# A hybrid decoder trunk: probabilities turned as one tile, gate sums by scans on VectorE, and a fifth weight buffer

## The chip, the cores and the metric

The kernel runs on one core of one Trainium2 chip. The metric is the device time of one execution in microseconds (us). The core has TensorE (PE, matrix products), VectorE (DVE), ScalarE (ACT), GpSimd (POOL) and SyncE (SP); SP, ACT and POOL also issue DMAs, which 16 DMA engines carry out.

## What is computed

The trunk has two layers over 256 rows of width 2048. In each layer the input is normalised and multiplied with one wide matrix (`w_in`), whose columns feed four groups of four heads; the groups' outputs, each times its own SiLU gate, are concatenated, multiplied with `w_out` and added to the input. One more normalisation follows the last layer.

```
h = rms_norm(x, norm_g);  p = split_columns(h @ w_in)
fox  = softmax(q.k/sqrt(d) + F[t] - F[s], causal) v,   F = cumsum(log_sigmoid(f))
diff = (softmax(q1.k1) - lam * softmax(q2.k2)) v, then rms_norm
moba = softmax(q.k, causal) v        (one block of 256 keys, so all of it is the own block)
gla  = sum over s <= t of (q_t * exp(C[t] - C[s])) . k_s v_s, then rms_norm
       C = cumsum(log_sigmoid(a @ wa + ba)) / 16, for each of 64 features of a head
x = x + concat(fox, diff, moba, gla, each * silu(gate)) @ w_out
```

Everything is float32.

## The kernel before

**Weights.** Each product with `w_in` or `w_out` is made in blocks of up to 512 columns and in steps of two or four 128-row pieces. A step loads 512 KB of weights from memory into a `raw` buffer (`load`, L1116, on SP's queue, `RAW_BUFS` = 4 of them), splits them into a part `hi` on ACT (`hi_of`, L414) and a rest `lo` on DVE (`lo_of`, L417), and multiplies: activations are also split in two (`hTp`, or `mTh` and `mTl`), and three products hi·hi, lo·hi, hi·lo add up in PSUM (`multiply`, L1196; an ordinary step is 12 matmuls of 512 columns). Parts are made three steps ahead (`ahead`, L1249).

**Order.** The order of all instructions on every engine is written by the program itself. The main loop (L1282) goes through the steps; behind each step `tick` (L263) lets every pending task go on to its next `yield`. Tasks are Python generators: `gla`, `fox`, `diff`, `moba`, the `run` that follows a projection, `make_hT` at the layer's end. So a `yield` means "behind the next step of 12 matmuls". `tick` stops when a rough count of the DVE or ACT time given out exceeds what PE has had (`Costed`, L169; `give_time`, L1242). A step that needs something not ready yet forces ticks (L1290).

**Buffers.** Working tiles come from numbered slots: `four` (4 KB a partition, `T4` = 10), `two` (2 KB, `T2` = 6), `eight` (one), `gate` (two) and `side` (two, in PSUM). `take` waits in steps for a free one.

**Turning.** A 128x128 transpose of float32 data is made off PE: DVE transposes 32x32 blocks (`turned`, L289), and two DMA hops on POOL's queue put the blocks in their places by way of DRAM (`moved`, L303): the first hop writes a tile `turn`, two yields later four DMAs read it back, and three yields later the tile counts as landed. The softmax probabilities of a group are two tiles, of the first 128 queries (4 blocks, in a `two` slot) and of the second (8 blocks, in a `four` slot); `turned_p` (L775) turns both as two jobs, which makes 2 + 8 DMAs. In MoBA and FoX the product of probabilities and values (`attend_columns`, L794) reads the turned tiles directly; in diff they are copied first (L984).

**GLA.** `gla` (L625) needs exp of differences of the running sum C at seven levels of halving blocks, for both halves of 128 rows, and two whole-half sums. Before, each is a sum of log gates over a set of rows: a constant matrix `a_r` of nine 128x128 sets is multiplied with the log gates, split in hi and lo (`gh`, `glo`), on PE (L661 to L672), and ACT takes exp out of PSUM into `ee` (L674). Then DVE multiplies with q and k (L683 to L696) and PE makes the products of `ee` and `tq` (L701).

**The layer's end.** `make_hT` (L447) turns the new `xs` into the next layer's `hTp` in four chunks; the first three by `moved`, the last by PE transposes (`turn_x`, L426). The output projection takes its inputs in the order GLA, FoX, diff, MoBA.

Of the kernel before, what the change touches and what calls it, by code (L numbers as in the profile page):

```python
# [21 lines left out]
P = 128  # L22
# [11 lines left out]
NEG = -1.0e30  # L34
RAW_BUFS = 4
PART_BUFS = 4
WARM = 10
X_AT = (24, 28, 32, 36)
T4 = 10
T2 = 6  # L40
STEP_W = 1056
# [21 lines left out]
def _constants():  # L63

    i = np.arange(P)
    tables, at = {"f": [], "b": []}, {}

    def put(name, a, kind="f"):
        parts = tables[kind]
        at[name] = (sum(x.shape[1] for x in parts), a.shape[1])  # L70
        parts.append(np.ascontiguousarray(a, TYPES[kind]))

    put("ident", np.eye(P))
    put("after", (i[:, None] > i[None, :]))
# [9 lines left out]
    sets, masks = [], []  # L84
    for h in GLA_LEVELS:
        blk, second = i // (2 * h), (i // h) % 2 == 1
        ref = blk * 2 * h + h - 1
        u, t = i[:, None], i[None, :]
        a = np.where(second[None, :], (u > ref[None, :]) & (u <= t), (u > t) & (u <= ref[None, :]))
        sets.append(a / GLA_TAU)  # L90
        masks.append(((blk[:, None] == blk[None, :]) & ~second[:, None])[:, second])
    sets += [(i[:, None] > i[None, :]) / GLA_TAU, (i[:, None] <= i[None, :]) / GLA_TAU]
    put("sets", np.concatenate(sets, 1), "b")
    put("masks", np.concatenate(masks, 1), "b")
    return {k: np.concatenate(v, 1) for k, v in tables.items()}, at
# [115 lines left out]
def hybrid_trunk(  # L211
# [30 lines left out]

    s4 = Slots(wk, "four", T4)
    s2 = Slots(wk, "two", T2)
    s8 = Slots(wk, "eight", 1)
    sgs = Slots(wk, "gate", 2)
# [41 lines left out]

    def turned(jobs, release):  # L289

        made = []
        for src, slots, inner in jobs:
            n = src.shape[1]
            t = yield from slots.take([P, 4, n, 32] if inner == "j" else [P, 4, 32, n])
            v_.transpose(t.rearrange("p c n j -> p n c j" if inner == "j" else "p c j n -> p n c j"),
                         src.rearrange("p n (c i) -> p n c i", c=4))
            made.append(t)
        release()
        yield
        yield from moved(made)  # L300
        return made

    def moved(made):  # L303

        via = []
        for t in made:
            n = t.shape[2] * t.shape[3]
            via.append(dram.tile([P, 4, n], F32, name=f"turn{n}", tag=f"turn{n}", bufs=4))
            g_.dma_start(via[-1], t.rearrange("p c a b -> p c (a b)"))  # L309
        yield  # L310
        yield
        for t, z in zip(made, via):
            for c in range(4):
                g_.dma_start(t[c * 32:(c + 1) * 32].rearrange("p q a b -> p q (a b)"), z[:, c].rearrange("(q i) e -> i q e", q=4))  # L314
        yield
        yield
        yield

# [16 lines left out]
    ones_r = cp.tile([P, P], F32R, name="ones_r")  # L335
    a_r = cp.tile([P, (NL + 2) * P], F32R, name="a_r")
    neg_b = cp.tile([P, P], BF16, name="neg_b")
# [23 lines left out]
    def constants():  # L361
# [5 lines left out]
        s = []  # L367
        for name in ("sets", "upto", "masks"):
# [11 lines left out]
        yield  # L380
        v_.tensor_copy(a_r, s[0])
        v_.tensor_copy(upto_r, s[1])
        v_.tensor_copy(masks.rearrange("p l t -> p (l t)"), s[2])
        v_.tensor_scalar(ones_r, ident, 0.0, 1.0, op0=OP.mult, op1=OP.add)
# [62 lines left out]
    def make_hT(l, chunk, parts):  # L447
        if chunk < 3:
            yield
        if l == 1 and chunk < 2:  # L450
# [3 lines left out]
            for _ in range(4):  # L454
                yield
        if chunk == 3:
            ps = yield from take_side()
            turn_x(ps, chunk)
            yield
            split_x([ps[:, k * 256:(k + 1) * 256].rearrange("p (m t) -> p m t", m=2) for k in range(4)], l, chunk)  # L460
            side.put(ps)
            yield
            squares(l, chunk, parts)
            return
# [3 lines left out]
        for m in range(2):  # L468
            v_.transpose(tk[:, m], x4[:, m].rearrange("p k (c i) -> p k c i", c=4))
        yield  # L470
        squares(l, chunk, parts)
        yield from moved([t])
        tk = t.rearrange("p q j (k m) -> p k m (q j)", m=2)
# [30 lines left out]
    def projected(name, pool=None, heads_first=False, func=AF.Copy, turn=None, natural=None):  # L504
# [7 lines left out]
        def run(l, nat):  # L512
            yield
            if turn is not None:
                yield from rotated(nat, *turn)
            t, = yield from turned([(nat, pool or s4, "j")], lambda: s4.put(nat))
            if natural:
# [39 lines left out]
    def finish_rows(l, gi, o, ops, scale, sg):  # L557
# [20 lines left out]
        yield  # L578
        t, = yield from turned([(mixed.rearrange("p h m d -> p (h m) d"), s4, "j")], lambda: s4.put(mixed))
        z = yield from natural_of(t, s4, ((slice(None), gain[:, 0 if gi == 1 else 1, l:l + 1]),))  # L580
# [44 lines left out]
    def gla(l, an):  # L625
        yield from until("constants")
        ps = yield from take_side()
        for m in range(2):
# [5 lines left out]
        al = yield from take_side()  # L634
        for m in range(2):
            matmul(al[:, m * 256:(m + 1) * 256], at17[:, m * P:(m + 1) * P], wa[:, l], True, True)
        yield
        e = yield from s2.take([P, 512])
        gl = yield from s2.take([P, 2, 256])
        yield from log_sigmoid(gl.rearrange("p m e -> p (m e)"), al[:, :512], e)  # L640
        s2.put(e)
        side.put(al)
        yield
        gh = yield from s2.take([P, 2, 256], F32R)
        hi_of(gh, gl)
        yield
        glo = yield from s2.take([P, 2, 256], F32R)
        lo_of(glo, gl, gh)
        s2.put(gl)
# [9 lines left out]
        for pair in range(2):  # L659
            ee = yield from s8.take([P, 2, NL + 1, P])  # L660
            for m in range(2):  # L661
                pe = yield from take_side()
                for b in range(2):
                    for part in (gh, glo):
                        lhs = part[:, m, pair * P:(pair + 1) * P]
                        if b == 0:
                            matmul(pe[:, :512], lhs, a_r[:, 0:512], part is gh, part is glo)
                        elif m == 0:
                            matmul(pe[:, 512:], lhs, a_r[:, 512:1024], part is gh, part is glo)
                        else:  # L670
                            matmul(pe[:, 512:896], lhs, a_r[:, 512:896], part is gh, False)
                            matmul(pe[:, 896:], lhs, a_r[:, (NL + 1) * P:], False, part is glo)  # L672
                yield
                a_.activation(ee[:, m].rearrange("p l t -> p (l t)"), pe, AF.Exp)  # L674
                side.put(pe)
            yield

# [40 lines left out]
        s4.put(env["gla_qk", l])  # L718
        s2.put(gh, glo)
        yield from until(("gla_v", l))  # L720
# [53 lines left out]

    def turned_p(p0, p1, inner, pool0=s2, slot0=None):  # L775

        def release():
            pool0.put(p0 if slot0 is None else slot0)
            s4.put(p1)

        t0, t1 = yield from turned([(p0, s2, inner), (p1.rearrange("p h j s -> p (h j) s"), s4, inner)], release)
        return t0, t1

    def normalised(p0, p1, su):
# [6 lines left out]
        yield  # L791
        return (yield from turned_p(p0, p1, "j"))

    def attend_columns(l, gi, name, qT, kT, forget=None):  # L794
# [3 lines left out]
        yield  # L798
        t0, t1 = yield from normalised(p0, p1, su)
        yield from until((name + "_v", l))  # L800
# [5 lines left out]
        for h in range(H):  # L806
            v0, v1 = vn[:, 0, h * P:(h + 1) * P], vn[:, 1, h * P:(h + 1) * P]
            matmul(o[:, h, :P], v0, t0[:, :, h], True, True)
            matmul(o[:, h, P:], v0, t1[:, :, 2 * h], True, False)
            matmul(o[:, h, P:], v1, t1[:, :, 2 * h + 1], False, True)  # L810
        s4.put(t1, vn)
        s2.put(t0)
        yield
# [94 lines left out]
    def diff(l):  # L908
# [73 lines left out]
        s4.put(p1[1])  # L982
        t0, t1 = yield from turned_p(p0[:, 0], p1[0], "j", s4, p0)
        z0 = yield from natural_of(t0, s2)  # L984
        z1 = yield from natural_of(t1, s4)
        yield
# [343 lines left out]
```

## Time and profile before

| | |
|---|---|
| runs, us | 942.41, 937.63, 938.47 (median 938.47) |
| the profiled execution, us | 939.94; its span from the first to the last instruction 938.1 |
| busy: PE, DVE, ACT, POOL, us | 917.3, 577.6, 505.5, 120.5 |
| DMA | 204.56 MB, 218 GB/s on average |
| granted clock of PE, mean | 0.991 |

The profile is of one execution. Its first part gives each engine's busy time and share of the span. Lines of groups and of the timeline read: start or group, engine, operation, tile written `<-` tiles read, shapes, number of instructions, and in square brackets the idle time before the instruction and who ended it. Buffer numbers are left out, so `four` is any tile in a `four` slot; `gate<-turn` is the second hop of a tile in a `gate` slot.

### The profile page before, as it was taken

The numbers are of one execution on the slowest core, as the hardware profiler recorded it, in microseconds if no ns is written. First come the engines' busy times: TensorE is split into PE (matmuls) and PEld (weight loads), VectorE is DVE, ScalarE is ACT, GpSimd is POOL, SyncE is SP. The second block draws the span as 40 slices with busy tenths as digits, with TensorE's granted clock in tenths as the row PEclk, the third lists the DMA queues.
The fourth block names the chain that finished last, engine by engine and source line by source line (L and its number), as shares of the span: only waits on it lengthen the run. The fifth ranks groups of instructions, "written<-read, shape, count | busy, mean of one in ns | idle before, by whom it ended". The sixth has DMA issues, their size and how long they took to land.

```text
span 938.1 us, 12710 instructions
## 1 busy us (share of the span) xinstructions
PE 917.3 (98%) x4734; PEld 780.8 (83%) x4734; DVE 577.6 (62%) x782; ACT 505.5 (54%) x712; POOL 120.5 (13%) x204
## 2 busy tenths in 40 slices
PE   9999999999999999899999999999999999989996
PEld 7979888898888888788898888888988888868886
DVE  7664876674755576456754548866657555655563
ACT  7586654455644555345646567446465545733441
POOL 0010011220121123001200100022301112140000
PEclk9999999999999999999999999999999999998998
DMA  9856576788786767678855855678967777696652
GB/s 315 273 174 224 166 233 193 247 250 242 222 235 217 242 204 243 199 219 262 272 172 169 243 153 187 179 213 245 273 193 255 229 222 217 200 283 208 190 169 90
DMA packets 60271, 204.56 MB, mean 218 GB/s; under 512 B 8977, under 2 KB 9265, under 8 KB 60210
## 3 DMA queue, kind: packets, MB, share of 16 engines
q1 hardware_dynamic: 46048, 164.20, 55.9%
q0 software_dynamic: 12528, 37.76, 14.4%
q10 hardware_dynamic: 1634, 1.80, 0.6%
q8 instruction: 37, 0.61, 0.3%
q14 instruction: 24, 0.20, 0.1%
HBM read 183.80 MB, written 19.92 MB: 217 GB/s over the span
## 4 chain that ended last, share of the span: by engine, by line
PE 88%; DMA 5%; issue 3%; POOL 1%; DVE 1%; ACT 1%; POOLq 0%; DVEq 0%; ACTq 0%
PE mm L282 78%; PE side L282 10%; DMA four<-turn 2%; DMA gate<-turn 2%; DMA turn<-four 1%; POOL four L314 1%; PE side L354 0%; DVE lo L181 0%; ACT hi L181 0%; DVE xs L181 0%; POOL gate L314 0%; ACT L181 0%; DVE four L181 0%; ACT hTp L181 0%; PE side L286 0%
## 5 line engine op out<-in xcount | busy, mean ns | idle before, releaser
L181 DVE TENSOR_TENSOR lo<-raw,hi 128x1024 fp32r<-128x1024 f32 (+3 forms) x301 | 366.2, 1220 | 315.0 <-ACT hi L181 314.4
L181 ACT ACTIVATE hi<-raw 128x1024 fp32r<-128x1024 f32 (+3 forms) x301 | 317.3, 1059 | 378.8 <-PE mm L282 318.4
L282 PE MATMUL mm<-hi,hTp 128*128 128x512 f32 (+2 forms) x2048 | 465.8, 371 | 0.0
L282 PEld LDWEIGHTS mm<-hi,hTp 128*128 128x128 f32 x2048 | 358.7, 188 | 66.3 <-issue 1.1
L282 PE MATMUL mm<-lo,hTp 128*128 128x512 f32 (+2 forms) x1024 | 249.8, 369 | 0.0
L282 PEld LDWEIGHTS mm<-lo,hTp 128*128 128x128 f32 x1024 | 181.0, 188 | 32.7
L282 PE MATMUL mm<-hi,mTh 128*128 128x512 f32 (+1 forms) x256 | 95.7, 379 | 0.0
L282 PE MATMUL mm<-hi,mTl 128*128 128x512 f32 (+1 forms) x256 | 95.3, 377 | 0.0
L314 POOL DMA_DIRECT2D four<-turn x108 | 59.2, 554 | 76.7 <-DMA turn<-four 38.6
L282 PE MATMUL mm<-lo,mTh 128*128 128x512 f32 (+1 forms) x256 | 64.4, 376 | 0.0
L309 POOL DMA_DIRECT2D turn<-four x27 | 15.4, 569 | 348.0 <-DVE four L181 337.9
L282 PEld LDWEIGHTS mm<-hi,mTl 128*128 128x128 f32 x256 | 48.5, 189 | 9.0 <-DVE mTl L181 0.3
L282 PEld LDWEIGHTS mm<-hi,mTh 128*128 128x128 f32 x256 | 48.5, 189 | 8.8
L282 PEld LDWEIGHTS mm<-lo,mTh 128*128 128x128 f32 x256 | 46.2, 188 | 8.8
L282 PE MATMUL side<-four,four 128*128 128x128 f32 (+1 forms) x320 | 40.2, 289 | 7.8 <-DMA four<-turn 7.8
L282 PEld LDWEIGHTS side<-four,four 128*128 128x128 f32 (+1 forms) x320 | 37.1, 202 | 10.4 <-issue 9.5
L181 ACT ACTIVATE four<-mm,rstd 128x512 f32<-128x512 f32 (+2 forms) x56 | 33.6, 647 | 3.6 <-DVE fx L181 3.6
L181 ACT ACT_TABLE_LOAD x26 | 33.4, 1283 | 3.3 <-DVE an L181 3.0
L181 DVE STREAM_TRANSPOSE four<-four 128x1024 f32<-128x1024 f32 x24 | 29.6, 1232 | 0.3
L181 ACT ACTIVATE four<-side,nb 128x256 f32<-128x256 f32 (+1 forms) x48 | 20.5, 436 | 2.0 <-DVE nb L181 1.9
L181 DVE COPY_PREDICATED four<-masks,side 128x128 f32<-128x128 uint8 x56 | 19.1, 341 | 1.8
L181 ACT ACTIVATE two<-xs 128x512 f32<-128x512 f32 (+1 forms) x18 | 10.3, 571 | 14.6 <-DVE xs L181 14.6
(144 smaller groups left out, 525.3 us busy)
## 6 DMA issues: line engine op xcount, KB each, us to landing
raw<-in_weights SPq DMA_DIRECT2D x272, 512.0 KB, 4.2
turn<-four POOLq DMA_DIRECT2D x27, 512.0 KB, 4.4
four<-turn POOLq DMA_DIRECT2D x108, 128.0 KB, 5.4
raw<-in_weights SPq DMA_DIRECT2D x16, 516.0 KB, 4.8
raw<-in_weights SPq DMA_DIRECT2D x15, 528.0 KB, 4.9
turn<-gate POOLq DMA_DIRECT2D x4, 512.0 KB, 5.2
gate<-turn POOLq DMA_DIRECT2D x16, 128.0 KB, 5.6
four<-in_xt SPq DMA_DIRECT2D x3, 512.0 KB, 6.3
```

The lines of the kernel that those rows point to most:

```text
L181: return f(*args, **kw)
L282: t_.matmul(out, lhsT, rhs, start=start, stop=stop)
L309: g_.dma_start(via[-1], t.rearrange("p c a b -> p c (a b)"))
L314: g_.dma_start(t[c * 32:(c + 1) * 32].rearrange("p q a b -> p q (a b)"), z[:, c].rearrange("(q i) e -> i q e", q=4))
```

## The change

- **Turned probabilities.** The two tiles of probabilities become parts of one tile of 12 blocks in a slot of their own kind, `six` (6 KB, `T6` = 1): one first hop and four second hops, 5 DMAs instead of 10. In exchange `T4` goes from 10 to 9 and `T2` from 6 to 5. In diff the copies read the parts of the one tile.
- **Steps of a turn.** `moved` begins in the step of the transposes (the yield behind `release` goes), has one yield between its hops and then five (`LAND`), for every turn. In `make_hT` the yield ahead of the squares goes; its last chunk gets one yield ahead of its PE transposes.
- **GLA.** One yield more at the start. The logits are made with features on the partitions (operands of the two matmuls exchanged). The log gates' running sums are four scans on DVE; for each pair of heads, each level is one subtraction of the value at the block's middle, and two more operations make the whole-half sums; ACT takes Abs and then exp with a scale of -1/16. The products with `a_r` go, as do the split of the log gates, the constant and its load.
- **Weights.** `RAW_BUFS` goes from 4 to 5.

```diff
-RAW_BUFS = 4
+RAW_BUFS = 5
-T4 = 10
-T2 = 6
+T4 = 9
+T2 = 5
+T6 = 1
+LAND = 5
...
-    def turned(jobs, release):
-        made = []
-        for src, slots, inner in jobs:
...
-        release()
-        yield
-        yield from moved(made)
-        return made
+    def turned(sources, slots, release):
+        n = sum(s.shape[1] for s in sources)
+        t = yield from slots.take([P, 4, n, 32])
+        at = 0
+        for src in sources:
+            k = src.shape[1]
+            v_.transpose(t[:, :, at:at + k].rearrange("p c n j -> p n c j"), src.rearrange("p n (c i) -> p n c i", c=4))
+            at += k
         release()
+        yield from moved(t)
+        return t
+    def moved(t):
+        n = t.shape[2] * t.shape[3]
+        via = dram.tile([P, 4, n], F32, name=f"turn{n}", tag=f"turn{n}", bufs=4)
+        g_.dma_start(via, t.rearrange("p c a b -> p c (a b)"))
+        yield
+        for c in range(4):
+            g_.dma_start(t[c * 32:(c + 1) * 32].rearrange("p q a b -> p q (a b)"), via[:, c].rearrange("(q i) e -> i q e", q=4))
+        for _ in range(LAND):
+            yield
...
         if chunk == 3:
+            yield
             ps = yield from take_side()
...
-        yield
         squares(l, chunk, parts)
-        yield from moved([t])
+        yield from moved(t)
...
     def gla(l, an):
         yield from until("constants")
+        yield
         ps = yield from take_side()
...
-        for m in range(2):
-            matmul(al[:, m * 256:(m + 1) * 256], at17[:, m * P:(m + 1) * P], wa[:, l], True, True)
+        for pair in range(2):
+            matmul(al[:, pair * SEQ:(pair + 1) * SEQ], wa[:, l, pair * P:(pair + 1) * P], at17, True, True)
...
-        gh = yield from s2.take([P, 2, 256], F32R)
-        hi_of(gh, gl)
-        yield
-        glo = yield from s2.take([P, 2, 256], F32R)
-        lo_of(glo, gl, gh)
+        cum = yield from s2.take([P, 2, SEQ])
+        for pair in range(2):
+            for m in range(2):
+                c = slice(m * P, (m + 1) * P)
+                v_.tensor_tensor_scan(cum[:, pair, c], gl[:, pair, c], gl[:, pair, c], 0.0, op0=OP.add, op1=OP.bypass)
...
+            for i, h in enumerate(GLA_LEVELS):
+                src = cum[:, pair].rearrange("p (m b w) -> p m b w", m=2, w=2 * h)
+                v_.tensor_sub(ee[:, :, i].rearrange("p m (b w) -> p m b w", w=2 * h), src,
+                              src[:, :, :, h - 1:h].to_broadcast([P, 2, 64 // h, 2 * h]))
+                if i == 3:
+                    yield
+            v_.tensor_scalar(ee[:, 0, NL], cum[:, pair, :P], cum[:, pair, P - 1:P], None, op0=OP.subtract)
+            v_.tensor_copy(ee[:, 1, NL], cum[:, pair, P:])
+            yield
             for m in range(2):
-                pe = yield from take_side()
...
-                            matmul(pe[:, :512], lhs, a_r[:, 0:512], part is gh, part is glo)
...
+                a_.activation(ee[:, m], ee[:, m], AF.Abs)
+                a_.activation(ee[:, m], ee[:, m], AF.Exp, scale=-1.0 / GLA_TAU)
                 yield
-                a_.activation(ee[:, m].rearrange("p l t -> p (l t)"), pe, AF.Exp)
-                side.put(pe)
-            yield
...
-        t0, t1 = yield from turned([(p0, s2, inner), (p1.rearrange("p h j s -> p (h j) s"), s4, inner)], release)
-        return t0, t1
+        return (yield from turned([p0, p1.rearrange("p h j s -> p (h j) s")], s6, release))
...
-            matmul(o[:, h, :P], v0, t0[:, :, h], True, True)
-            matmul(o[:, h, P:], v0, t1[:, :, 2 * h], True, False)
-            matmul(o[:, h, P:], v1, t1[:, :, 2 * h + 1], False, True)
+            matmul(o[:, h, :P], v0, t[:, :, h], True, True)
+            matmul(o[:, h, P:], v0, t[:, :, H + 2 * h], True, False)
+            matmul(o[:, h, P:], v1, t[:, :, H + 2 * h + 1], False, True)
...
```

More of the change, by code (lines that the diff above doesn't have):

```diff
@@ L83, in _constants @@
     put("neg", np.where(i[None, :] > i[:, None], NEG, 0.0), "b")
-    sets, masks = [], []
+    masks = []
     for h in GLA_LEVELS:
         blk, second = i // (2 * h), (i // h) % 2 == 1
[L87 to L90, printed above, removed]
         masks.append(((blk[:, None] == blk[None, :]) & ~second[:, None])[:, second])
-    sets += [(i[:, None] > i[None, :]) / GLA_TAU, (i[:, None] <= i[None, :]) / GLA_TAU]
-    put("sets", np.concatenate(sets, 1), "b")
     put("masks", np.concatenate(masks, 1), "b")
@@ L244, in hybrid_trunk @@
     s2 = Slots(wk, "two", T2)
+    s6 = Slots(wk, "six", T6)
     s8 = Slots(wk, "eight", 1)
@@ L286, in transpose @@
         t_.transpose(out, src, ident)
-    def turned(jobs, release):
-        made = []
-        for src, slots, inner in jobs:
[L293 to L297, printed above, removed]
-        release()
-        yield
-        yield from moved(made)
-        return made
[L303 to L309, printed above, removed]
-        yield
-        yield
-        for t, z in zip(made, via):
-            for c in range(4):
-                g_.dma_start(t[c * 32:(c + 1) * 32].rearrange("p q a b -> p q (a b)"), z[:, c].rearrange("(q i) e -> i q e", q=4))
-        yield
-        yield
-        yield
+    def turned(sources, slots, release):
[6 more added lines that the diff above has]
+            at += k
+        release()
+        yield from moved(t)
[4 more added lines that the diff above has]
+        g_.dma_start(via, t.rearrange("p c a b -> p c (a b)"))
+        yield
+        for c in range(4):
+            g_.dma_start(t[c * 32:(c + 1) * 32].rearrange("p q a b -> p q (a b)"), via[:, c].rearrange("(q i) e -> i q e", q=4))
+        for _ in range(LAND):
+            yield
     ct = cp.tile([P, CONST["f"].shape[1]], F32, name="ct")
@@ L335, in hybrid_trunk @@
     ones_r = cp.tile([P, P], F32R, name="ones_r")
-    a_r = cp.tile([P, (NL + 2) * P], F32R, name="a_r")
     neg_b = cp.tile([P, P], BF16, name="neg_b")
@@ L367, in constants @@
         s = []
-        for name in ("sets", "upto", "masks"):
+        for name in ("upto", "masks"):
             c, n = CAT[name]
@@ L380, in constants @@
         yield
-        v_.tensor_copy(a_r, s[0])
-        v_.tensor_copy(upto_r, s[1])
-        v_.tensor_copy(masks.rearrange("p l t -> p (l t)"), s[2])
+        v_.tensor_copy(upto_r, s[0])
+        v_.tensor_copy(masks.rearrange("p l t -> p (l t)"), s[1])
         v_.tensor_scalar(ones_r, ident, 0.0, 1.0, op0=OP.mult, op1=OP.add)
@@ L469, in make_hT @@
             v_.transpose(tk[:, m], x4[:, m].rearrange("p k (c i) -> p k c i", c=4))
-        yield
         squares(l, chunk, parts)
-        yield from moved([t])
+        yield from moved(t)
         tk = t.rearrange("p q j (k m) -> p k m (q j)", m=2)
@@ L515, in run @@
                 yield from rotated(nat, *turn)
-            t, = yield from turned([(nat, pool or s4, "j")], lambda: s4.put(nat))
+            t = yield from turned([nat], pool or s4, lambda: s4.put(nat))
             if natural:
@@ L578, in finish_rows @@
         yield
-        t, = yield from turned([(mixed.rearrange("p h m d -> p (h m) d"), s4, "j")], lambda: s4.put(mixed))
+        t = yield from turned([mixed.rearrange("p h m d -> p (h m) d")], s4, lambda: s4.put(mixed))
         z = yield from natural_of(t, s4, ((slice(None), gain[:, 0 if gi == 1 else 1, l:l + 1]),))
@@ L634, in gla @@
         al = yield from take_side()
-        for m in range(2):
-            matmul(al[:, m * 256:(m + 1) * 256], at17[:, m * P:(m + 1) * P], wa[:, l], True, True)
+        for pair in range(2):
+            matmul(al[:, pair * SEQ:(pair + 1) * SEQ], wa[:, l, pair * P:(pair + 1) * P], at17, True, True)
         yield
         e = yield from s2.take([P, 512])
-        gl = yield from s2.take([P, 2, 256])
-        yield from log_sigmoid(gl.rearrange("p m e -> p (m e)"), al[:, :512], e)
+        gl = yield from s2.take([P, 2, SEQ])
+        yield from log_sigmoid(gl.rearrange("p x t -> p (x t)"), al[:, :512], e)
         s2.put(e)
@@ L643, in gla @@
         yield
-        gh = yield from s2.take([P, 2, 256], F32R)
-        hi_of(gh, gl)
-        yield
-        glo = yield from s2.take([P, 2, 256], F32R)
-        lo_of(glo, gl, gh)
+        cum = yield from s2.take([P, 2, SEQ])
[3 more added lines that the diff above has]
+                v_.tensor_tensor_scan(cum[:, pair, c], gl[:, pair, c], gl[:, pair, c], 0.0, op0=OP.add, op1=OP.bypass)
         s2.put(gl)
@@ L660, in gla @@
             ee = yield from s8.take([P, 2, NL + 1, P])
-            for m in range(2):
-                pe = yield from take_side()
[L663 to L666, printed above, removed]
-                            matmul(pe[:, :512], lhs, a_r[:, 0:512], part is gh, part is glo)
[L668 to L672, printed above, removed]
+            for i, h in enumerate(GLA_LEVELS):
[7 more added lines that the diff above has]
+            yield
+            for m in range(2):
+                a_.activation(ee[:, m], ee[:, m], AF.Abs)
+                a_.activation(ee[:, m], ee[:, m], AF.Exp, scale=-1.0 / GLA_TAU)
                 yield
-                a_.activation(ee[:, m].rearrange("p l t -> p (l t)"), pe, AF.Exp)
-                side.put(pe)
-            yield
             def half(z, h, second):
@@ L718, in gla @@
         s4.put(env["gla_qk", l])
-        s2.put(gh, glo)
+        s2.put(cum)
         yield from until(("gla_v", l))
@@ L773, in softmax, with turned_p @@
         return p
-    def turned_p(p0, p1, inner, pool0=s2, slot0=None):
+    def turned_p(p0, p1, pool0=s2, slot0=None):
         def release():
@@ L791, in normalised @@
         yield
-        return (yield from turned_p(p0, p1, "j"))
+        return (yield from turned_p(p0, p1))
     def attend_columns(l, gi, name, qT, kT, forget=None):
@@ L798, in attend_columns @@
         yield
-        t0, t1 = yield from normalised(p0, p1, su)
+        t = yield from normalised(p0, p1, su)
         yield from until((name + "_v", l))
@@ L807, in attend_columns @@
             v0, v1 = vn[:, 0, h * P:(h + 1) * P], vn[:, 1, h * P:(h + 1) * P]
-            matmul(o[:, h, :P], v0, t0[:, :, h], True, True)
-            matmul(o[:, h, P:], v0, t1[:, :, 2 * h], True, False)
-            matmul(o[:, h, P:], v1, t1[:, :, 2 * h + 1], False, True)
-        s4.put(t1, vn)
-        s2.put(t0)
+            matmul(o[:, h, :P], v0, t[:, :, h], True, True)
+            matmul(o[:, h, P:], v0, t[:, :, H + 2 * h], True, False)
+            matmul(o[:, h, P:], v1, t[:, :, H + 2 * h + 1], False, True)
+        s4.put(vn)
+        s6.put(t)
         yield
@@ L982, in diff @@
         s4.put(p1[1])
-        t0, t1 = yield from turned_p(p0[:, 0], p1[0], "j", s4, p0)
-        z0 = yield from natural_of(t0, s2)
-        z1 = yield from natural_of(t1, s4)
+        t = yield from turned_p(p0[:, 0], p1[0], s4, p0)
+        z0 = yield from s2.take([P, H, P])
+        z1 = yield from s4.take([P, 2 * H, P])
+        for z, part in ((z0, t[:, :, :H]), (z1, t[:, :, H:])):
+            a_.activation(z.rearrange("p n (q j) -> p n q j", q=4), part.rearrange("p q n j -> p n q j"), AF.Copy)
+        s6.put(t)
         yield
```

## The prediction

> **What bounds the kernel now.** I read the page's first part, then the list of what TensorE (PE) waits for, then the chain of waits in order of time. The columns of the first two are busy time with its share, and the sum, number and longest of a wait.
>
> ```profile
> span 938.1 us, 12710 instructions
> PE 917.3 (98%) x4734; PEld 780.8 (83%) x4734; DVE 577.6 (62%) x782; ACT 505.5 (54%) x712; POOL 120.5 (13%) x204
> ```
>
> ```profile
> PE side L282 <- DMA four<-turn: 7.8, 2, 4.1
> PE side L286 <- DVE an L181: 1.5, 2, 0.8
> PE side L286 <- DVE xs L181: 1.4, 2, 1.1
> PE side L282 <- DVE eight L181: 0.3, 1, 0.3
> ```
>
> ```profile
> 86.05 0.93 PE side L282 x4
> ...
> 337.79 2.68 PE side L282 x24
> 340.46 21.68 PE mm L282 x96
> ...
> 583.75 0.99 PE side L282 x6
> ```
>
> PE is the bound, at 98%. An ordinary step of 12 matmuls takes 2.71 us (96 in 21.68), and no line of the waits has raw, hi or lo in it: the weights are always there in time. So only three things count: matmuls that disappear, the waits listed above, and new waits. Work on VectorE (DVE, 62%) and ScalarE (ACT, 54%) is free until PE waits for it.
>
> The waits for `four<-turn` are the two places (one per layer) where MoBA's product of probabilities and values needs the turned probabilities. PE's timeline shows both, with start, duration and the idle time before:
>
> ```profile
> 378.43 0.38 PE L282 MATMUL side<-two,four 128*128 128x128 f32 x2
> 382.54 1.19 PE L282 MATMUL side<-four,four 128*128 128x128 f32 x4 [3.72 <-DMA four<-turn]
> ...
> 386.49 0.48 PE L282 MATMUL mm<-hi,mTh 128*128 128x512 f32 x1
> ...
> 839.33 0.38 PE L282 MATMUL side<-two,four 128*128 128x128 f32 x2
> 843.78 1.19 PE L282 MATMUL side<-four,four 128*128 128x128 f32 x4 [4.07 <-DMA four<-turn]
> ...
> 848.46 0.77 PE L282 MATMUL mm<-hi,mTh 128*128 128x512 f32 x1
> ```
>
> These 24 matmuls take 8.06 us (378.43 to 386.49) and 9.13 us, where the same 24 take 2.68 elsewhere: 5.4 and 6.4 lost, 11.8 in all, more than the waits alone. The rest is the clock, in the table of stretches (the granted clock is the third number from the end):
>
> ```profile
> 382.00:386.00 4.00, 3.46 (x17) 3.50 (x18) 0.93 (x1) 0.00 (x0) 0.00 (x0) 0.57 0.88 336
> 844.00:848.00 4.00, 4.00 (x20) 4.00 (x21) 1.23 (x1) 0.61 (x1) 0.00 (x0) 0.50 1.03 404
> 468.00:472.00 4.00, 2.61 (x21) 2.21 (x21) 3.43 (x4) 1.42 (x3) 0.00 (x0) 1.00 0.44 132
> ```
>
> After waits of 3.72 and 4.07 us the clock is at about half; with a wait of 1.1 (468) it stays at 1.00.
>
> **The matmuls removed: -7.7 us.** Per layer and pair of heads, groups of 4 and 6 matmuls on `a_r` go, at 0.93 and 0.99 us: two pairs, two layers, 4 x (0.93 + 0.99) = 7.7. Nothing is added on PE; the gate's logits are two matmuls as before, with the operands exchanged.
>
> **Two later steps: -2.9 us.** One step more ahead of the transposes of `an` and of the last chunk of `xs` puts 12 matmuls (2.71 us) between, more than the longest wait there (1.1). Both waits, 1.5 + 1.4, go. The hidden cost: the last chunk is wanted by PE six steps later, so one step is covered; GLA's result is wanted only in the output projection, dozens of steps later.
>
> **VectorE and ScalarE in GLA.** The prices:
>
> ```profile
> L181 DVE TENSOR_TENSOR two<-four,ct 128x256 f32<-128x256 f32 x8 | 3.3, 418 | 0.0
> L181 ACT ACTIVATE eight<-side 128x1024 f32<-128x1024 f32 x8 | 8.2, 1023 | 0.9 <-PE side L282 0.8
> ```
>
> Per layer DVE gets 14 subtractions of 256 elements at 0.418 = 5.9 us, and four operations of 128 and four scans of 128. The page of before has no scan; no reason makes it dearer than a 256-element operation, so 0 to 0.418 each for the eight, 3.3 at most: 9.2. ACT gets four Abs of 1024 at 1.023 = 4.1. (The split of gl into hi and lo goes; I leave out the credit.) Where they fall, in stretches before the two pairs' products (columns PE, weight load, DVE, ACT):
>
> ```profile
> 88.00:92.00 4.00, 4.00 (x28) 3.69 (x27) 1.38 (x3) 2.05 (x3) 0.00 (x0) 1.00 0.36 134
> 120.00:124.00 4.00, 4.00 (x21) 3.38 (x20) 1.56 (x2) 4.00 (x8) 0.00 (x0) 1.00 0.57 216
> ```
>
> DVE is idle 2.4 of 4 us in both, which takes a pair's share of 4.6 over two such stretches. ACT is full in the second, and runs late there; its cover is the weight parts, made three steps (8.1 us) ahead. The nearest price of being late is the one wait of 0.3 for `eight` now, in four pairs. I take 0.25 for each of the four: +1.0, with 0 and 3 as ends.
>
> **The turned probabilities.** From the transposes to the use there are six yields as before (1 + 5 instead of 1 + 2 + 3), so MoBA's product stays at the same place in PE's order. What moves is the queue of GpSimd (POOL), which issues these DMAs in order: a turn's second hop comes one step after the first, not two. POOL's timeline in layer 0, and three lines of layer 1:
>
> ```profile
> 359.04 0.56 POOL L309 DMA_DIRECT2D turn<-gate  x1 [11.22 <-DVE gate L181]
> 362.45 0.56 POOL L309 DMA_DIRECT2D turn<-two  x1 [2.85 <-DVE two L181]
> 363.57 0.54 POOL L309 DMA_DIRECT2D turn<-four  x1 [0.56 <-DVE four L181]
> 364.28 2.20 POOL L314 DMA_DIRECT2D gate<-turn  x4 [0.17 <-issue]
> ...
> 369.73 0.55 POOL L314 DMA_DIRECT2D two<-turn  x1 [1.16 <-DMA turn<-four]
> 371.65 1.21 POOL L314 DMA_DIRECT2D four<-turn  x2 [1.36 <-DMA gate<-turn]
> ...
> 819.63 0.56 POOL L309 DMA_DIRECT2D turn<-gate  x1 [10.93 <-DVE gate L181]
> 823.33 0.56 POOL L309 DMA_DIRECT2D turn<-two  x1 [3.14 <-DVE two L181]
> 824.46 0.54 POOL L309 DMA_DIRECT2D turn<-four  x1 [0.57 <-DVE four L181]
> ```
>
> The waits at 369.73 and 371.65 are for DMAs that these don't read: each is for the eighth issue before it (gate, two, four, then four times each). The merged tile makes 10 issues of these 15, and the eighth before is then an old one: this wait goes. But the gate's second hop moves ahead of the probabilities' first, and POOL waits in between for the gate's first to land. Times to landing, from the DMA issues of these stretches (layer 0, then layer 1, and the last for diff's turn with less beside it):
>
> ```profile
> turn<-gate POOLq DMA_DIRECT2D x1, 512.0 KB, 5.0
> turn<-four POOLq DMA_DIRECT2D x1, 512.0 KB, 5.9
> four<-turn POOLq DMA_DIRECT2D x4, 128.0 KB, 7.3
> ...
> turn<-gate POOLq DMA_DIRECT2D x1, 512.0 KB, 3.6
> turn<-four POOLq DMA_DIRECT2D x1, 512.0 KB, 4.0
> ...
> four<-turn POOLq DMA_DIRECT2D x4, 128.0 KB, 5.2
> ```
>
> Layer 0: the gate's first hop lands at 359.04 + 5.0 = 364.0, its second is issued by 366.2, and then the 768 KB of probabilities start, 3.8 us later than now. The same bytes took 362.45 to 363.57 + 5.9 = 7.0 us, and 5.1 in layer 1. So they land at 371.3 to 373.2; the last of four issues starts 1.65 later and lands after 5.2 to 7.3: 378.2 to 382.2. PE asks at 378.43, so it waits 0 to 3.7. Layer 1 by the same sum: 823.2, 825.4, 830.5 to 832.4, 837.4 to 841.4; PE asks at 839.33 and waits 0 to 2.0. As the DMA engines are full here (0.88 and 1.03 in the stretches above, next to last number) I take the later halves, 2.2 and 1.2. Both lie nearer to the 1.1 that kept the clock than to 3.72, so I leave the clock at full: -11.8 + 3.4 = -8.4.
>
> The Trainium skill (TensorE: Matmul & The Clock Gate, Part 1) says that PE falls to half rate after an idle window of about 3.4 us, which is free-running. The trace agrees for 3.72 and 4.07 us; by it 2.2 costs no clock either.
>
> A new wait: diff's transposes write the single `six` slot that fox's product has just read.
>
> ```profile
> 263.71 0.61 PE L282 MATMUL side<-four,four 128*128 128x128 f32 x4
> ```
>
> ```profile
> 260.58 0.70 DVE L181 STREAM_TRANSPOSE two<-four 128x512 f32<-128x512 f32 x1
> ```
>
> They start 3.7 us later (264.3 instead of 260.58), and the lo of a later step is queued behind them on DVE; it is made three steps ahead, 8.1 us, so it costs nothing. Squares one step earlier, fewer slots and constants: off the path. The fifth raw buffer: nothing by itself, as PE never waits for weights.
>
> **The sum.** -7.7 - 2.9 - 8.4 + 1.0 = -18.0 us. The profiled execution took 939.94 us around its span of 938.1; the median of the runs is 938.47. From that: 920.5.
>
> **The rivals.**
> (a) The DMA engines are the limit of the hops, whoever is ahead in the queue: 2.1 MB go through beside the weights either way, the engines are full, and the probabilities start 3.8 us later. Then 11.8 stays: 938.47 - 7.7 - 2.9 + 1.0 = 928.9. For it: the shares of 1.03; against: POOL's waits above, which were not for bytes. 0.18.
> (b) The waits vanish: 938.47 - 7.7 - 2.9 - 11.8 + 1.0 = 917.1. For it: the lower ends of both sums are 0; against: those need the quickest hop of the trace in its fullest stretch. 0.14.
> The Trainium skill (DMA: Bandwidth & Descriptors, Anatomy of one DMA) gives 2.0 us plus bytes at 436 GB/s for such a DMA, which would bring the probabilities in before PE asks and give this time. The trace disagrees: a 512 KB hop took 5.0 and 5.9 us here, not 3.2.
> (c) Slower: GLA's vector work becomes the bound. 9.2 + 4.1 = 13.3 us a layer, 26.6 in all, on engines that are full near the products; on the path in full beside (a) it gives 927.9 + 26.6 = 954.5. It decides once DVE or ACT falls more than three steps (8.1 us) behind PE, and it is slower than before when over 10.6 of the 26.6 show. Against: the idle shares above. 0.03.
> (d) The kernel does what it says but most of it is given back: 934 to 943, by (a) with half of (c). 0.07.
> Forecast: 0.58.
>
> **The numbers.** A difference within 0.5% (4.7 us) is no change for this kernel's measurement. Forecast, (a) and (b) are all faster: 0.58 + 0.18 + 0.14 = 0.90; (d) mostly the same, 0.07; slower 0.03. The range holds the forecast, (a) with GLA's upper price (928.9 + 2 = 930.9) and (b) without any GLA price (916.1) less the 1.5 by which the profiled execution differs from the median: 914.5 to 931.
>
> **What would show it.** Right: no `a_r` matmuls and no waits of PE for `an` or `xs`; MoBA's 24 matmuls in under 5 us in both layers with the clock at 1.00; POOL issuing the probabilities' first hop right behind the gate's second, and no wait for the eighth DMA before. Wrong: these matmuls still taking 8 to 9 us (a), or PE waiting for lo, hi or `eight` between 80 and 150 us and 540 and 610 us (c).

## The result and the profile after

The changed kernel takes 954.21 us (median of 4 runs, 950.59 to 956.26) beside 938.05 of the kernel before: the ratio is 1.0146, interval [1.0121, 1.0172]. It is slower by 1.5%; 920.5 was forecast. The profiled execution took 954.34 us, its span is 951.9. The head of its page, and what PE waited for (sum, number, longest):

```profile
span 951.9 us, 12619 instructions
PE 927.1 (97%) x4694; PEld 776.0 (82%) x4694; DVE 589.3 (62%) x823; ACT 512.1 (54%) x718; POOL 104.0 (11%) x174
```

```profile
PE side L279 <- DMA six<-turn: 7.6, 2, 4.4
PE side L279 <- DVE eight L177: 4.9, 2, 3.1
PE side L279 <- DMA four<-turn: 1.7, 1, 1.7
```

PE has 40 matmuls fewer and is busy 9.8 us longer. The waits for `an` and `xs` are gone. MoBA's wait has the same size as before (7.6 beside 7.8) under a new name, and its 24 matmuls behind it still run at a low clock, 4.54 and 5.14 us in the chain instead of 2.68:

```profile
389.44 4.54 PE side L279 x24
...
856.60 5.14 PE side L279 x24
```

The wait for `eight` has grown from 0.3 to 4.9, and one for `four<-turn` is new: diff's first product waits for its turned keys. All waits together grew by only some 3 us. The rest is in no list of waits. It is in the chain, in a stretch of 216 plain matmuls (18 steps, nothing between), first of the kernel before, then of the changed one; columns are start, duration, what:

```profile
749.70 48.98 PE mm L282 x216
```

```profile
760.25 50.19 PE mm L279 x216
```

That is 226.8 ns from matmul to matmul before and 232.4 after, 5.6 ns more. The largest group by form (busy, mean ns of one), before and after:

```profile
L282 PE MATMUL mm<-hi,hTp 128*128 128x512 f32 x1664 | 414.7, 391 | 0.0
```

```profile
L279 PE MATMUL mm<-hi,hTp 128*128 128x512 f32 x1664 | 424.1, 397 | 0.0
```

All five groups with 512 columns of weights have a longer mean. The 256 matmuls of the same operands with 258 columns are busy 33.4 us at a mean of 283 ns in both traces, so it isn't the clock (0.991 before, 0.990 after). The program has 3,168 matmuls with 512 columns of weights (1,664 + 832 + 3 x 224 in the groups): 3,168 x 5.6 ns = 17.7 us. The balance of the two profiled spans: +17.7, -7.7 (`a_r`), -2.9 (`an`, `xs`), +4.6 (`eight`), +1.7 (diff), -0.2 (MoBA), +1.1 (clock: 0.9% of 938.1 before, 1.0% of 951.9 after) = +14.3, measured +13.8.

So there were three questions: why plain matmuls take longer, why MoBA's wait stayed, and where the new waits in GLA and diff come from.

### The profile page after: what moved, and what is told of

It is laid out like the page before. It is cut to its first block, busy times and chain, and to the rows that moved or that the text cites. A ratio compares the mean times of both kernels' runs of the same rounds, so it can differ in the third digit from the quotient of the medians.

```text
span 951.9 us, 12619 instructions
## 1 busy us (share of the span) xinstructions
PE 927.1 (97%) x4694; PEld 776.0 (82%) x4694; DVE 589.3 (62%) x823; ACT 512.1 (54%) x718; POOL 104.0 (11%) x174
## 3 DMA queue, kind: packets, MB, share of 16 engines
q0 software_dynamic: 11664, 37.76, 13.8%
## 4 chain that ended last, share of the span: by engine, by line
PE 89%; DMA 3%; ACT 2%; DVE 2%; issue 2%; POOL 1%; SPq 0%; POOLq 0%; DVEq 0%; ACTq 0%
PE mm L279 80%; PE side L279 9%; DMA six<-turn 2%; ACT hi L177 1%; DVE lo L177 1%; DVE tq L177 1%; ACT eight L177 1%; DMA four<-turn 1%; DMA four<-in_xt 1%; POOL six L306 0%; ACT four L177 0%; DVE xs L177 0%; ACT L177 0%; POOL four L306 0%; PE side L283 0%
## 5 line engine op out<-in xcount | busy, mean ns | idle before, releaser
L279 PE MATMUL mm<-hi,hTp 128*128 128x512 f32 (+2 forms) x2048 | 475.1, 376 | 0.6 <-DVE hTp L177 0.4
L279 PE MATMUL mm<-lo,hTp 128*128 128x512 f32 (+2 forms) x1024 | 254.9, 374 | 0.1
L306 POOL DMA_DIRECT2D four<-turn x84 | 46.0, 554 | 85.2 <-DMA turn<-four 44.6
L303 POOL DMA_DIRECT2D turn<-four x21 | 12.2, 581 | 334.6 <-DVE four L177 334.6
L177 ACT ACT_TABLE_LOAD x26 | 33.4, 1283 | 3.3 <-DVE an L177 3.0
L279 PEld LDWEIGHTS side<-four,four 128*128 128x128 f32 (+1 forms) x256 | 26.1, 190 | 4.2 <-issue 3.3
L279 PE MATMUL side<-four,four 128*128 128x128 f32 (+1 forms) x256 | 27.8, 277 | 1.7 <-DMA four<-turn 1.7
L279 PE MATMUL side<-six,four 128*128 128x128 f32 x96 | 15.4, 333 | 7.6 <-DMA six<-turn 7.6
L177 DVE STREAM_TRANSPOSE four<-four 128x1024 f32<-128x1024 f32 x18 | 22.3, 1241 | 0.3
L279 PEld LDWEIGHTS side<-six,four 128*128 128x128 f32 x96 | 15.0, 247 | 8.6 <-issue 8.4
```

The source lines that it names most:

```text
L177: return f(*args, **kw)
L279: t_.matmul(out, lhsT, rhs, start=start, stop=stop)
L303: g_.dma_start(via, t.rearrange("p c a b -> p c (a b)"))
```

## The experiments

Times are medians, ratios are to the kernel before in the same runs; the clock is the mean granted one of the profiled execution.

| kernel | us (runs) | ratio, interval | span, clock |
|---|---|---|---|
| e1: changed, hi and lo moved by 128 bytes | 945.47 (10) | 1.0049 [1.0024, 1.0075] | 947.2, 0.982 |
| e2: before, hi and lo moved by 128 bytes | 952.6 (4) | 1.0122 [1.0067, 1.0177] | 949.3, 0.995 |
| e3: e1 with four raw buffers | 950.62 (4) | 1.0103 [1.0039, 1.0168] | 953.5, 0.988 |
| e4: the turns alone | 939.05 (10) | 0.999 [0.996, 1.0021] | 933.8, 0.994 |
| e5: the scans alone | 941.7 (10) | 1.0013 [0.999, 1.0037] | 940.2, 0.987 |
| e6: e1, GLA's product two steps later | 929.44 (4) | 0.9881 [0.9848, 0.9914] | 928.5, 0.993 |
| e7: e1, two steps between the hops | 937.77 (10) | 0.9969 [0.9951, 0.9988] | 931.5, 0.991 |
| e8: e6 and e7, MoBA's product a step later | 924.77 (4) | 0.9835 [0.9805, 0.9864] | 922.2, 0.995 |
| e9, e10, e11: before, other places | 942.82, 951.98, 948.82 (1 each) | | 941.0, 950.1, 947.0 |
| e12: e6 and e7, MoBA's gate held | 920.68 (6) | 0.9798 [0.9765, 0.983] | 919.0, 0.996 |
| e13: e12 with four raw buffers | 920.97 (4) | 0.9794 [0.9773, 0.9815] | 919.1, 0.996 |
| e14: e13 with GLA's sums by `a_r` | 928.71 (6) | 0.9876 [0.9856, 0.9895] | 927.0, 0.996 |

### Where the weights lie: e1, e2, e3

Other long stretches of the changed kernel's chain, of 204 and of 128 plain matmuls, have the same 232.4 ns from one to the next, whatever DVE, ACT and the DMAs do there, so I looked at what is constant: addresses. In the memory map `a_r` (4,608 bytes a partition, 18 times 256) went from ahead of the activations, and a fifth `raw` of 4,224 bytes came between them and `hi`. Before, `hTp` begins at 39,296 and `hi` at 121,728; after, at 34,688 and 121,344. The edit of all three experiments:

```diff
         raw = wst.tile([P, STEP_W], F32, name="raw", bufs=RAW_BUFS)
+        if i == 0:
+            gap = wst.tile([P, 32], F32, name="gap", bufs=1)
+            nc.vector.memset(gap, 0.0)
```

> The changed kernel with a tile of 128 bytes a partition between the raw weights and their parts hi and lo (and one memset of it at the start), so that hi and lo begin at a multiple of 256 bytes plus 128, as in the kernel before; nothing else differs. Theory (the place of hi and lo sets how fast a matmul with 512 columns follows the last): its start-to-start time falls back from 232.4 ns to 226.7 ns, 3,168 of them times 5.7 ns are 18 us, so 933 to 940 us. Rival (the fifth raw buffer, or what it lets the loads do, slows TensorE): 232.4 ns stay and 951 to 957 us.

> The kernel before with the same tile of 128 bytes at the same place, so that hi and lo begin at a multiple of 256 bytes, as in the changed kernel; nothing of the change is in it. Theory (place): 226.7 ns become 232 to 233.5 ns and the time rises by 17 to 21 us, to 954 to 960 us. Rival (some part of the change itself): no difference, 936 to 941 us.

> The changed kernel with four raw buffers, and the tile of 128 bytes, so that hi and lo begin at a multiple of 256 bytes as in the changed kernel. Theory (place): still 232.4 ns, 951 to 957 us. Rival (the fifth raw buffer): back to 226.7 ns, 933 to 940 us.

The same stretch of the chain in e1 and in e2:

```profile
757.34 48.98 PE mm L279 x216
```

```profile
760.17 50.18 PE mm L282 x216
```

e3 takes 50.18 as well. The 128 bytes alone make the changed kernel's matmuls fast again, and those of the kernel before slow with nothing of the change in it; four buffers at the bad place stay slow. The place is the cause, not the traffic of a fifth buffer. The times follow with less than 17.7 us: +12.6 in e2, -8.7 in e1. So e1 lies above the range of its theory, and e2 and e3 lie just below theirs. Slower matmuls give transfers and vector work more time, and the stalls shrink: e2 waits 6.0 us for `four<-turn` instead of 7.8 and 0.4 for `xs` instead of 1.4, and by the spans it spends 4.7 us in lost clock (0.5% of 949.3) where the kernel before spends 8.4.

e1 is the changed kernel without that cost, and it is still slower than the one before by 0.49%. Its waits of PE, and the stretch behind GLA's wait in layer 0 (the granted clock is the third number from the end):

```profile
PE side L279 <- DMA six<-turn: 9.4, 2, 5.7
PE side L279 <- DVE eight L177: 5.8, 2, 3.6
PE side L279 <- DMA four<-turn: 5.0, 3, 2.3
```

```profile
106.00:109.00 3.00, 2.49 (x17) 2.52 (x18) 3.00 (x12) 3.00 (x9) 0.00 (x0) 0.79 0.55 162
```

The clock is down to 0.79 there, and to 0.68 from 225 to 231 us, at diff's wait: both waits now cost clock too. With a mean of 0.982 over 947.2 us, 17.0 us of clock are lost, 8.6 more than before.

### Only the distance counts: e9, e10, e11

My theory so far was that `hi` and `lo` must not begin at a multiple of 256 bytes. The rival, that their distance from the activations decides, gives the same in e1 to e3. A tile of 128 bytes behind the constants moves both:

```diff
+    far = cp.tile([P, 32], F32, name="far")
+    nc.vector.memset(far, 0.0)
     xs = big.tile([P, 2, D], F32, name="xs")
```

> The kernel before with a tile of 128 bytes behind the constants, so that the activations (hTp, mTh, mTl) and hi and lo all move by 128 bytes and begin at multiples of 256 bytes. Theory (the place of hi and lo alone decides): 232 to 233.5 ns from one matmul with 512 columns to the next, about 952 us. Rival (the distance between weights and activations decides, modulo 256 bytes; it is 0 as in the kernel before): 226.7 ns, 937 to 943 us.

> The kernel before with both tiles of 128 bytes, behind the constants and between raw and hi: the activations begin at multiples of 256 bytes, hi and lo at a multiple plus 128. Theory (the place of hi and lo alone decides): 226.7 ns, 937 to 943 us. Rival (the distance decides; it is 128 as in the changed kernel): 232 to 233.5 ns, about 952 us.

> The kernel before with a tile of 64 bytes between raw and hi: hi and lo begin at a multiple of 256 bytes plus 192. If only a begin at a multiple of 256 bytes is slow, 226.7 ns and 937 to 943 us; if only the begin at 128 past it is fast, over 230 ns and about 950 us.

The stretch of 216 in e9, e10 and e11:

```profile
753.60 48.98 PE mm L282 x216
```

```profile
761.50 50.18 PE mm L282 x216
```

```profile
757.89 49.46 PE mm L282 x216
```

| | activations begin at, modulo 256 | hi and lo | distance | ns from matmul to matmul |
|---|---|---|---|---|
| before, e1 | 128 | 128 | 0 | 226.8 |
| e9 | 0 | 0 | 0 | 226.8 |
| e11 | 128 | 192 | 64 | 229.0 |
| changed, e2, e3 | 128 | 0 | 128 | 232.4, 232.3, 232.3 |
| e10 | 0 | 128 | 128 | 232.3 |

My theory fell: e9 begins at multiples of 256 bytes and is fast, e10 begins at 128 past one and is slow. The distance between the operand that is held in PE (activations) and the one that streams through (weights), modulo 256 bytes, decides, and in degrees: 64 bytes cost less than half of what 128 cost. The working slots behind `hi` and `lo` move along in all of these runs, but the plain matmuls don't read them. The Trainium skill (TensorE: Matmul & The Clock Gate, Step-by-step: what each phase is for) says that PE reads its two operands from SBUF through two independent ports. Ports that are independent in every respect would let neither operand's place matter to the other; here it changed the pace from 226.8 to 232.4 ns. Why it does so stays open.

It is shown for the weights against `hTp`, `mTh` and `mTl`. Of the few other matmuls with 512 columns, the eight that stream `four` past `upto_r` go the same way: a mean of 420 ns at a distance of 128 (before, e9), 412 and 411 at 0 (changed, e10). The four that stream `two` past `upto_r` go the other way, 392 and 397 ns, so for single matmuls among others the rule is not settled.

### The two halves of the change: e4, e5

e4 leaves out the scans, e5 everything but the scans; the distance is 0 in both, with four raw buffers.

> The changed kernel with the sums of log f by matmuls with a_r as before and four raw buffers: the one tile of probabilities, the five steps to land and the moved waits for an and xs are left of the change, and hi and lo lie where they did before. Theory (place, and MoBA's turn bound by its transfers, so that its wait only moves from two tiles to one): 226.7 ns, 933 to 938 us, MoBA's product still waits 7 to 9 us in all. Rival (the prediction's own step): MoBA's waits shrink by 8.4 us and the two others by 2.9 us, 925 to 930 us.

> The kernel before with one part of the change: the sums of log f by scans and subtractions, without a_r. Turns, waits for an and xs, four raw buffers and the places modulo 256 bytes of hi and lo are as before. Theory (of what the well placed changed kernel lost, GLA's own stage took only its waits for eight, 5.5 us, and the half clock behind them, 3.4 us, and gave 7.7 us back; diff's waits come from the order of the turns): 1 us above the kernel before, 939 to 943 us, and no wait of diff's first product for its turned keys. Rival (the longer vector work delays diff's and MoBA's turns too): 4 to 8 us above it, 943 to 948 us, with those waits.

e4 is level with the kernel before and 1 us above the theory's range: the turns and the two later steps together gave nothing, far from the rival's 925 to 930, and the two waits for `six<-turn` sum to 6.5 us. e5 is level too, as expected: 7.7 us of matmuls are paid back at `eight`.

```profile
PE side L276 <- DVE eight L175: 5.8, 2, 3.6
```

Beside it stand MoBA's wait of before (7.0 us) and none at diff, as the theory has it.

### The stalls one by one: e6, e7, e8

**GLA.** ACT's timeline in the changed kernel ahead of the first pair's product:

```profile
91.68 1.05 ACT L177 ACTIVATE eight<-eight 128x1024 f32<-128x1024 f32 x1
92.75 1.28 ACT L177 ACT_TABLE_LOAD   x1
94.04 1.06 ACT L177 ACTIVATE eight<-eight 128x1024 f32<-128x1024 f32 x1
95.01 1.04 ACT L177 ACTIVATE hi<-raw 128x1024 fp32r<-128x1024 f32 x1
95.96 2.14 ACT L177 ACTIVATE eight<-eight 128x1024 f32<-128x1024 f32 x2
```

and the end of the chain on DVE and PE (groups of DVE's timeline, then PE's):

```profile
100.22 2.38 DVE L177 TENSOR_TENSOR tq<-eight,four 64x128 f32<-64x128 f32 x8
...
107.03 1.50 DVE L177 TENSOR_TENSOR eight<-eight,four 128x128 f32<-128x128 f32 x7
```

```profile
107.47 3.36 PE L279 MATMUL side<-tq,eight 128*128 128x128 f32 x28 [1.81 <-DVE eight L177]
```

Abs, a table load, exp, Abs, exp, then DVE's products, one behind the other with weight parts between: the first product begins at 107.47, 15.8 us after the first Abs. DVE stood idle for 4.81 us of this, so it isn't full; the product stands too early in PE's order.

```diff
+            yield
+            yield
             both = yield from take_both()
```

> The well placed changed kernel (the one with the tile of 128 bytes), with two more steps between the last multiplication of eight and GLA's product. Theory (the product only stood too early for the new vector work): the waits for eight, 5.8 us, and 3.4 us of half clock go, 934 to 939 us. Rival (GLA's vector work is the bound of its stage, so the wait moves to what comes next on the slots of eight or side): 942 to 947 us.

```profile
PE side L279 <- DMA six<-turn: 10.7, 2, 6.5
```

This, and 1.3 us at the start of the kernel, are all that is left of e6's waits. The wait for `eight` is gone and came back nowhere. The gain, 16.0 us, is more than the 9 expected, because diff's waits went as well: the program's order shifts with the two steps, and diff's keys now leave ahead of fox's probabilities (on POOL their first hop `turn<-four` at 198.80, `turn<-six` at 205.71).

**diff and MoBA.** POOL's timeline in e1 and, below it, the time to landing of diff's first hop:

```profile
201.94 0.56 POOL L303 DMA_DIRECT2D turn<-six  x1 [20.35 <-DVE six L177]
206.34 1.10 POOL L306 DMA_DIRECT2D six<-turn  x2 [3.84 <-DMA turn<-six]
...
208.94 0.56 POOL L303 DMA_DIRECT2D turn<-four  x1
220.22 2.19 POOL L306 DMA_DIRECT2D four<-turn  x4 [10.72 <-issue]
```

```profile
turn<-four POOLq DMA_DIRECT2D x1, 512.0 KB, 10.7
```

With one step between its hops, fox's second hop (768 KB) stands ahead of diff's first, POOL waits 3.84 us in between, and diff's hop then takes 10.7 us. Two steps between, as before, turn the order round:

```diff
-LAND = 5
+LAND = 4
...
         g_.dma_start(via, t.rearrange("p c a b -> p c (a b)"))
         yield
+        yield
```

> The well placed changed kernel with two steps between a turn's first hop and its second, as before, and four behind it, six in all as in the changed kernel. Theory (with one step between, fox's second hop stands on POOL's queue ahead of diff's first one and the gate's second ahead of MoBA's first, and what stands behind a hop that waits is held up): diff's waits for its turned keys, 5.0 us, and the half clock behind them, 5.1 us, go, and MoBA's wait of 9.4 us shrinks by 2 to 4 us: 929 to 937 us. Rival (the transfers themselves are the bound in both places, whatever their order): 942 to 947 us, the same waits.

```profile
200.71 0.56 POOL L303 DMA_DIRECT2D turn<-six  x1 [20.23 <-DVE six L177]
204.30 0.56 POOL L303 DMA_DIRECT2D turn<-four  x1 [3.03 <-DVE four L177]
205.10 0.57 POOL L307 DMA_DIRECT2D six<-turn  x1 [0.25 <-DMA turn<-six]
```

```profile
turn<-four POOLq DMA_DIRECT2D x1, 512.0 KB, 4.4
```

```profile
PE side L279 <- DMA six<-turn: 6.2, 2, 3.7
```

diff's hop takes 4.4 us and its wait is gone; MoBA's fell by 3.2 as the theory had it. The median fell by 7.7 us, a little less than the 8.5 to 16.5 expected.

> Both edits of the two kernels before this one, and MoBA's product one step later. Theory (three stalls that come from where a step stands, each mended by itself): 945.5 less 9 in GLA, 10 at diff and 5 to 8 at MoBA is 918 to 923 us. Rival (the engines or transfers behind the stalls are bounds, and what is taken away in one place comes back in the next): 930 to 940 us.

e8 comes to 924.77, 1.8 us above the theory's 918 to 923 and far from the rival. MoBA's wait nearly went, but its product, a step later, now made the output projection wait for `mTl`:

```profile
PE mm L279 <- DVE mTl L177: 4.9, 2, 2.5
PE side L279 <- DMA six<-turn: 1.5, 2, 0.8
```

### The mended kernel and what its parts are worth: e12, e13, e14

In e8 the gate's second hop is still issued ahead of the probabilities' second. e12 puts MoBA's product back and holds that hop two steps longer (`hold` is the number of steps between the hops, 4 for MoBA's gate and 2 elsewhere):

```diff
-        yield
-        yield
+        for _ in range(hold):
+            yield
         for c in range(4):
...
-        for _ in range(LAND):
+        for _ in range(LAND + 2 - hold):
```

> The kernel with the three edits, with MoBA's product back at the changed kernel's step and the second hop of MoBA's gate held two steps longer, so that on POOL's queue it stands behind the second hop of the probabilities. Theory (the 512 KB of the gate's second hop stand ahead of the probabilities' and make them late by some 2 us): PE's waits for six and mTl, 6.4 us with the three edits, fall to 2 to 4 us, no half clock there, 919 to 923 us. Rival (the probabilities' own two hops are the bound): the wait for six grows to 5 us or more, half clock included 925 to 931 us.

```profile
353.33 0.56 POOL L304 DMA_DIRECT2D turn<-gate  x1 [10.30 <-DVE gate L178]
358.46 0.55 POOL L304 DMA_DIRECT2D turn<-six  x1 [4.56 <-DVE six L178]
363.71 2.21 POOL L308 DMA_DIRECT2D six<-turn  x4 [4.70 <-ACT hi L178]
365.91 2.18 POOL L308 DMA_DIRECT2D gate<-turn  x4
```

```profile
turn<-six POOLq DMA_DIRECT2D x1, 768.0 KB, 4.7
```

```profile
374.61 2.92 PE L280 MATMUL side<-six,four 128*128 128x128 f32 x24 [1.14 <-ACT hi L178]
...
825.68 4.54 PE L280 MATMUL side<-six,four 128*128 128x128 f32 x24 [2.75 <-DMA six<-turn]
```

Both waits of MoBA's product have shrunk, to 1.14 and 2.75 us, and nothing waits for `mTl`. The profile puts the first one down to ACT, but ACT's part was done at 373.66; the last of the four second hops was issued at 365.4, and the slowest hop of the tile took 9.0 us to land, which is 374.4. The second wait still cost clock (0.57 from 826 to 830 us), which the theory had ruled out. At 920.68 us the kernel beats both others, 2.0% faster than before.

> The mended kernel (three edits, MoBA's gate held) with four raw buffers in place of five and without the tile of 128 bytes, which leaves hi and lo at the same distance from the activations, modulo 256 bytes. Theory (the fifth buffer is worth nothing, as the prediction put it): the same time, 919 to 923 us. Rival (it covers late weights): 924 us or more, with waits for raw.

> The mended kernel with four raw buffers and GLA's sums of log f by matmuls with a_r again, as in the kernel before; hi and lo at the same distance. Theory (the prediction's two terms hold once no stall hides them: 7.7 us of matmuls come back, 1.0 us of vector work goes): 6 to 8 us above the kernel with four buffers and the scans, 926 to 930 us. Rival (GLA's scans are worth nothing): 919 to 923 us.

Both came as the theory said: the fifth buffer is worth nothing (920.97 beside 920.68), and the scans are worth 928.71 - 920.97 = 7.7 us once no stall hides them. (e14 leaves out e6's two later steps as well; nothing waits for `eight` in it.)

## Why the prediction was wrong, step by step

**The fifth raw buffer, put at nothing: the step that failed most.** As a buffer it is worth nothing (e13). As 4,224 bytes between the activations and the weight parts, 16.5 times 256, it moved the one against the other by 128 bytes and cost 17.7 us of matmuls (12.6 us of time, by e2). No rival had it; the only slower one was GLA's vector work, at 0.03.

**The matmuls removed and the two later steps: right.** The 40 matmuls and the waits for `an` and `xs` went.

**GLA's vector work, put at +1.0: wrong in size and place.** The prices were right. The groups of the changed kernel:

```profile
L177 ACT ACTIVATE eight<-eight 128x1024 f32<-128x1024 f32 x16 | 16.9, 1054 | 0.9 <-DVE eight L177 0.8
L177 DVE TENSOR_TENSOR eight<-two 128x256 f32<-128x256 f32 x28 | 10.0, 416 | 0.0
...
L177 DVE TENSOR_TENSOR_SCAN two<-two 128x128 f32<-128x128 f32 x8 | 2.7, 403 | 0.0
```

1,054 beside 1,023, 416 beside 418, and a scan 403, inside its bounds. What failed was the question. I asked whether ACT and DVE keep up with the weight parts, which have three steps of cover, and they do. The one without cover is PE's product of `eight` itself: it came just in time before (a wait of 0.3), so every link added to its chain shows. 4.9 us of waits came of it, 5.8 at full pace with the clock behind them. For the same reason rival (c)'s point of decision, three steps behind, was wrong.

**MoBA's turn, put at -8.4: wrong; rival (a) came true.** The waits are 3.2 and 4.4 us, where 2.2 and 1.2 were taken, and the 24 matmuls behind them take 4.54 and 5.14 us instead of 2.68. That makes 7.6 + 4.3 = 11.9 us, beside the 11.8 of before: nothing was gained. Two terms failed. The first is the time of the hops: the sum saw that the gate's second hop goes ahead of the probabilities' first, but gave the probabilities' hops the times that they had without it. The stretch of layer 0 after, on POOL's queue and to landing:

```profile
368.65 2.18 POOL L306 DMA_DIRECT2D gate<-turn  x4 [2.90 <-DMA turn<-gate]
370.81 0.56 POOL L303 DMA_DIRECT2D turn<-six  x1
378.49 2.18 POOL L306 DMA_DIRECT2D six<-turn  x4 [7.12 <-ACT hi L177]
```

```profile
turn<-six POOLq DMA_DIRECT2D x1, 768.0 KB, 7.1
six<-turn POOLq DMA_DIRECT2D x4, 192.0 KB, 8.0
```

The gate's first hop landed after 3.2 us, sooner than the 5.0 of the sum. But the probabilities' first hop took 7.1 us, and 9.1 in layer 1, where 5.1 to 7.0 was taken for both layers, and in layer 0 their second took 8.0, where up to 7.3 was. So the product began 24.2 and 25.5 us after the issue of the gate's first hop; the latest ends of the sum are 23.2 and 21.8. PE asked 1.7 and 1.4 us later than before, as its matmuls were slower, or the waits would be longer still.

The second term is the clock, which was left at full. Ahead of GLA's first product a wait of 2.2 us left it at 1.00 in e7, with 28 matmuls in 3.36 us, and lowered it to 0.62 in e1 (both from 107 to 110 us), with the same 28 in 4.99 us. At such lengths the length of the wait alone doesn't decide, and a step that counts on the full clock there counts on luck.

But (a)'s reason, that the DMA engines are the limit whoever is ahead, is refuted. In e7 the order alone took the waits from 9.4 to 6.2 us, and in e12 the engines are as full (0.92 to 1.05 from 354 to 378 us), but with the probabilities ahead of the gate's second hop their first hop takes 4.7 us in the same stretch, and the waits shrink from 7.6 to 3.9 us. The turns and the two later steps are worth 11.7 us then (e14 beside the kernel before, 940.36 in those runs), about the 8.4 + 2.9 of the prediction.

**diff's keys: missed.** The order on POOL's queue was worked out for MoBA's turn alone, though the same single step between the hops acts on every pair of turns that run together. fox's and diff's do; that cost 1.7 us of waits, 5.0 at full pace. The other new wait that was named, diff's transposes for `six`, did cost nothing.

e12 ends at 920.68, near the 920.5 forecast: about the sum's total came out once the weights lay right again and the new stalls were mended. That it ends so near is partly luck, as e12 changes three more places that the sum didn't know.

## What to carry to other kernels

A tile added or taken away moves every tile behind it: look at the memory map beside the diff, and when plain matmuls change their pace, move one operand by 128 bytes before anything else is explained. When steps between two DMAs on an in-order queue change, write the queue's new order down for every pair of turns that overlap, not only for the one that is meant. And where a product comes just in time, any work added to its chain shows in full, however idle the engines are on average; moving its place costs nothing if its result has slack.

## What the runs showed of the hardware

- Matmuls with 512 columns of 4 bytes follow each other after 226.8, 229.0 or 232.4 ns when streamed and held operand are 0, 64 or 128 bytes apart modulo 256; those with 258 columns kept their mean duration of 283 ns in both kernels. Other distances were not tried.
- A scan over 128 elements takes 403 ns on DVE, nearly as long as a subtraction of 256 (416).
- A first hop of 512 KB landed after 4.4 us when issued ahead of the 768 KB of another tile's second hop (e7), and after 10.7 us when issued behind them on the same queue (e1).
- After the same wait of 2.2 us in the same place the granted clock was 1.00 in one run (e7) and 0.62 in another (e1).
